# A mixture-of-experts trunk: the busiest expert changes places with the 13th, and that place gets 32 more slots

## The chip, the core and the metric

The kernel runs on one core of a Trainium2 chip. The metric is the device time of one execution in microseconds, a median over several runs. Engines are named as in the profile: PE (TensorE, with PEld its weight loads), DVE (VectorE), ACT (ScalarE), POOL (GpSimd), SP (SyncE, which issues all DMA loads here).

## The reference

One layer on 256 tokens of 1024 features, in float32: a norm, a mixer (differential attention beside a gated linear recurrence), a norm, and a mixture of 32 experts in which each token goes to the four best; then a last norm. The change lies in the experts:

```python
logits = (xt @ w_router).astype(jnp.float32) + b_router
top_v, top_e = lax.top_k(logits, TOP_K)
gates = jax.nn.softmax(top_v, axis=-1)
...
xb = xt[tok]
h = xb @ w_gu[e] + b_gu[e]
y = clamped_swiglu(h) @ w_down[e] + b_down[e]
return y * g[:, None].astype(y.dtype)
```

w_gu[e] is 1024 x 2048 (8 MB) and w_down[e] 1024 x 1024 (4 MB), so one expert has 12.58 MB (in units of 10^6 bytes). 256 tokens times 4 are 1024 places, 32 for an expert on average, and how many an expert really gets depends on the data.

## The kernel before

The first 120 us or so are the mixer and the router. `top4` makes the selection, `posm` holds for each token and expert the token's place in that expert's list, counted from 1 (0 if not selected), `gate` its weight, `cnt` the number of tokens of each expert. Then a loop over the experts runs, fully unrolled, each expert with CAP = 64 slots.

Weights arrive in chunks of 2 MB, six for an expert (`load_chunk`, L180): four of w_gu (h < NU, one DMA each) and two of w_down (two DMAs each). The order is that of `seq`: expert after expert, only for the last two experts all w_gu chunks come first. Ten buffers (`SLOTS`, six in one pool and four single ones) are used in turn; `ahead` (L1086) issues loads on SP up to ten chunks ahead of the use. PE and SP keep the order in which the code is written (`manual_schedule`); DVE, ACT and POOL are ordered by a scheduler.

For one expert e PE does, in this order:

- `gu_mm` (L863): for each 128 features k two products of 512 columns per half, h <- we, xg; 64 slots on half of the array's columns, so the two column halves g go side by side. These are 64 instructions of L875.
- `finish` (`combine`, L936): the products with the gates of the pair of experts before, added to `acc` by DVE.
- `act_t` (L891): transposes of the activation; between them `begin_gu` (L669) opens the next expert's accumulators with the bias.
- `need` (L1050): one half of the gather for the next pair of experts, as products with a 0/1 matrix S.
- `down_mm` (L902): y <- we, actT, 32 instructions of L908.

`swiglu` (L880) on DVE and ACT comes between the first and the third. The matrices S and the gates are built by POOL (`hot_rows`, `gate_rows`), pair by pair; the row `pick` that selects an expert's bias by ACT. After expert LATE = 13 `start_acc` (L1057) adds the residual and the down biases.

An expert with more than 64 tokens needs more than its slots. `plan` (L947), DVE's work at expert 1, counts how many blocks of 64 are missing (`todo_x`) and lists their experts. After the last expert's products and its combine (`fin`, L1145, into the accumulators `fps`) `extras` (L1041) runs nested branches, up to 15: a block (`extra`, L967) reads its expert's number into a register of SP, loads all six chunks of that expert again by that register (tiles wx), gathers, multiplies and adds to `fps`. The trace has one such block. Then `lnc` (the last norm's two rows) is loaded into buffer 5, and the last norm follows: BATCH_NORM_STATS2 on `fps` (L1193), their aggregate, the scaled rows, and the output in four DMAs.

`hint` (L681) marks for PE which way the first of these branches will go, from the count that L1154 loads into a register at the beginning of the last expert.

Of the kernel before, what the change touches and what calls it, by code (L numbers as in the profile page):

```python
# [23 lines left out]
NE = 32  # L24
CAP = 64
NX = 15
ALPHA = 2.0 ** 0.25
EPS = 1e-5
# [3 lines left out]
NW1 = 6  # L32
LATE = 13
NPRE = 4
# [13 lines left out]
def trunk(ctx, tc, x, ln0_g, ln0_b, w_in, conv_w, conv_b, w_rg_a, b_rg_a, w_rg_x, b_rg_x,  # L48
# [129 lines left out]
    seq += [(e, h) for e in (NE - 2, NE - 1) for h in range(NU, NH)]  # L178

    def load_chunk():  # L180


        i = nchunk[0]
        nchunk[0] += 1
        e, h = seq[i]
        w = wtile(f"we{e}_{h}", SLOTS[i % len(SLOTS)])
        if h < NU:
            SP.dma_start(w, w_gu[0, e].rearrange("(d p j) n -> p d (j n)", p=P, j=2)[:, h])
            for j in range(2):
                W[e, 2 * h + j] = w[:, j * 2 * D:(j + 1) * 2 * D]  # L190
            return
        for g in range(2):
            s = w_down[0, e].rearrange("(g b p j) n -> p g b (j n)", g=2, p=P, j=2)[:, g, h - NU]
# [472 lines left out]
    def open_pgu():  # L666
        pgu.append(sgu.enter_context(tc.tile_pool(name="pgu", bufs=3, space=PSUM, reuse_waits="tile")))

    def begin_gu(e, bs=range(2), pk=None):  # L669

        ps = begun.setdefault(e, {})
        if not ps:
            picks[e] = keep.tile([P, 2, CAP], F32R, tag="pick", bufs=2, name=f"pick{e}")
            src = pk[:, :, None] if pk is not None else two.rearrange("p (g c) -> p g c", g=2)[:, :, e:e + 1]
            A.activation(picks[e], src.to_broadcast([P, 2, CAP]), AF.Copy)
        for b in bs:
            ps[b] = pgu[-1].tile([P, 512], F32, tag="gu", name=f"h{e}_{b}")
            PE.matmul(ps[b], picks[e].rearrange("p g w -> p (g w)"), bgs[b], start=True, stop=False,  # L678
                      skip_group_check=True)
# [237 lines left out]
    def gate_rows(e):  # L917

        sg = wk.tile([P, NT, 3 * CAP], F32, tag="sgate", bufs=1, name=f"sgate{e}")
        for i in range(3):  # L920
            for t in range(NT):
                o = e + i % 2
                G.tensor_scalar(sg[:, t, i * CAP:(i + 1) * CAP], iota2[:, 0], posm[:, t, o:o + 1],  # L923
                                gate[:, t, o:o + 1], op0=OP.is_equal, op1=OP.mult)
        return sg
# [15 lines left out]

    start = keep.tile([P, NE], F32, name="start")
    upto = keep.tile([P, NE], F32, name="upto")
    posx = keep.tile([P, NT, NE], F32, name="posx")
    todo_x = keep.tile([1, NX + 1], I32, name="todo_x")

    def plan():  # L947


        xs = wk.tile([P, NE], F32, tag="sg", name="xs")  # L950
        V.tensor_scalar(xs, cnt, float(CAP), None, op0=OP.is_gt)
        for j in range(2, T // CAP):
            V.scalar_tensor_tensor(xs, cnt, float(j * CAP), xs, op0=OP.is_gt, op1=OP.add)
        V.tensor_tensor_scan(upto, ones[:, :NE], xs, 0.0, op0=OP.mult, op1=OP.add)
        V.tensor_sub(start, upto, xs)
        for t in range(NT):
            V.scalar_tensor_tensor(posx[:, t], start, float(CAP), posm[:, t], op0=OP.mult, op1=OP.add)
        le = wk.tile([1, NX, NE], F32, tag="l", bufs=2, name="le")
# [8 lines left out]
    def extra(i):  # L967

        key = f"x{i}"
        ex = nc.values_load(todo_x[0:1, i + 1:i + 2], engines=[ENG.SP], min_val=0, max_val=NE - 1)  # L970
        for h in range(NH):
            w = wtile(f"w{key}_{h}", SLOTS[nchunk[0] % len(SLOTS)] if i == 0 else 0)
            nchunk[0] += 1
            if h < NU:
                SP.dma_start(w, w_gu[0][bass.ds(ex, 1)].rearrange("o (d p j) n -> p (o d) (j n)", p=P, j=2)[:, h])
                for j in range(2):
                    W[key, 2 * h + j] = w[:, j * 2 * D:(j + 1) * 2 * D]
            else:
                src = w_down[0][bass.ds(ex, 1)].rearrange("o (g b p j) n -> p (o g) b (j n)", g=2, p=P, j=2)
                for g in range(2):  # L980
                    c = KT + 2 * (h - NU) + g
                    W[key, c] = w[:, g * 2 * D:(g + 1) * 2 * D]
                    SP.dma_start(W[key, c], src[:, g, h - NU])
        m = wk.tile([P, NE], F32, tag="mx", bufs=1, name=f"m{key}")
# [7 lines left out]
        V.tensor_scalar(pm, pm, -float((i + 1) * CAP), None, op0=OP.add)  # L992
        tmp = wk.tile([P, 2, NE], F32, tag="l", bufs=2, name=f"p{key}")
# [9 lines left out]
        xg = []  # L1003
        for half in range(2):
            xg.append(gather_tile(S, "g", f"{key}_{half}"))
            ps = mc("xg_ps")
# [7 lines left out]
        for t in range(NT):  # L1014
            PE.transpose(ps[:, t * P:(t + 1) * P], sg[:, t], ident)
        gt = wk.tile([P, 2, T], F32, tag="gtT", bufs=1, name=f"gtT{key}")[:, 0]
        A.activation(gt, ps[:, :T], AF.Copy)
# [6 lines left out]
        for b in range(2):  # L1024
            act_t(key, g, b, at[:, 2 * b:2 * b + 2])
        ps = dtiles(key)[0]
# [7 lines left out]
        y = ytile(key, 0)  # L1034
        A.activation(y, ps, AF.Copy)
        for t in range(NT):
            for n in range(2):
                ns = slice(n * CAP, (n + 1) * CAP)
                PE.matmul(fps[t][n], gt[ns, t * P:(t + 1) * P], y[ns], start=False, stop=True, skip_group_check=True)

    def extras(n, i=0):  # L1041
# [8 lines left out]
    def need(i, eng, half):  # L1050
        if i < len(GROUPS):
            es = GROUPS[i]
            if i not in xgs:
                xgs[i] = gather(es, CAP, posm[:, :, es[0]:es[-1] + 1], eng, "g")
            gather_mm(*xgs[i], half)
# [117 lines left out]
    for t in range(NT):  # L1173
        fin(t, gt, y, stop=True)
    extras(nx)
    lnw = wtile("lnc", 5)
# [66 lines left out]
```

## Time and profile before

| what | us |
|---|---|
| median of three runs | 1092.73 (1091.76 to 1093.57) |
| the profiled execution | 1092.81 |
| its span, first to last instruction | 1091.1 |
| PE busy in the span | 1005.0 (92%) |
| DVE, ACT, POOL busy | 281.6, 189.9, 147.2 |
| moved by DMA | 435.02 MB, mean 399 GB/s |

The page's second part cuts the span into 40 slices of 27.3 us. A list of waits has, for each engine and line, what it waited for, the total in us, how often, and the longest; SPq is the queue of SP, with its DMA issues. A row of a window has its ends, its length, and the busy time of PE, PEld, DVE, ACT and POOL with their instructions, the granted clock of PE, the DMA engines' busy share and GB/s. A timeline row has start, duration, engine, line, operation and tiles, and how long the engine stood before. A row by form has a bar, then the busy time and the mean of one instruction in ns, and a second bar with the idle time before. Where the rows of one line are listed, three numbers stand for the shortest, the median and the longest duration in ns. Tile names lose their numbers there: wx and hx belong to the extra block.

### The profile page before, as it was taken

The page shows a single profiled execution, that of the slowest core. Times are in us where ns is not written, and L with a number is a line of the kernel's source. Part 1 is how long each engine was busy: PE and PEld are TensorE (multiplying, and loading weights), DVE is VectorE, ACT ScalarE, POOL GpSimd, SP SyncE. Part 2 cuts the span into 40 slices and gives each one's busy share as a digit, 9 for nine tenths or more (in the row PEclk, how much of TensorE's full clock was granted, in tenths as well). Part 3 has the DMA queues.
Part 4 walks back from the last instruction along what each step waited for, and adds up shares of the span by engine and source line. Part 5 has one row for each costly group of instructions (what it writes and reads, how often), then busy time and mean ns, then how long its engine had stood idle before and what let it go on. Part 6 is the DMA issues. An engine that isn't in the chain of part 4 may idle for free. (4 is left out here: it accounts for less than half of the span.)

```text
span 1091.1 us, 12166 instructions
## 1 busy us (share of the span) xinstructions
PE 1005.0 (92%) x4904; PEld 455.8 (42%) x4904; DVE 281.6 (26%) x634; ACT 189.9 (17%) x429; POOL 147.2 (13%) x221
## 2 busy tenths in 40 slices
PE   8999999999999988989999988888888999888994
PEld 8987633444443332333343333333333333332341
DVE  6978413221211211115121212112011212121123
ACT  6675311111111010110111110100001111110011
POOL 4583202010110100101010101010010101010001
PEclk9999999999999999998999999999999999999997
DMA  8967799999999999999999999999999999999982
GB/s 282 323 258 327 294 412 428 427 426 425 424 427 424 424 427 424 424 425 426 427 427 424 426 426 423 427 426 422 425 425 426 427 426 425 426 425 427 424 357 80
DMA packets 48255, 435.02 MB, mean 399 GB/s; under 512 B 6493, under 2 KB 6558, under 8 KB 14528
## 3 DMA queue, kind: packets, MB, share of 16 engines
q1 hardware_dynamic: 48192, 434.17, 95.6%
q8 instruction: 41, 0.67, 0.3%
q14 instruction: 22, 0.18, 0.0%
HBM read 433.10 MB, written 1.05 MB: 398 GB/s over the span
## 5 line engine op out<-in xcount | busy, mean ns | idle before, releaser
L875 PE MATMUL h<-we,xg 128*64 128x512 f32 x2048 | 457.9, 595 | 55.8 <-DMA we<-in_w_gu_dram 55.1
L875 PEld LDWEIGHTS h<-we,xg 128*64 128x64 f32 x2048 | 145.0, 137 | 361.9 <-issue 290.7
L908 PE MATMUL y<-we,actT 128*64 128x512 f32 x1024 | 228.9, 599 | 0.0
L885 DVE TENSOR_SCALAR g<-h 128x256 f32<-128x256 f32 x64 | 27.2, 425 | 674.1 <-PE h L875 674.1
L923 POOL TENSOR_SCALAR sgate<-iota,posm,gate 128x64 f32<-128x64 f32 x96 | 54.6, 587 | 767.8 <-PE gt_ps L931 766.8
L908 PEld LDWEIGHTS y<-we,actT 128*64 128x64 f32 x1024 | 70.8, 137 | 135.3 <-issue 131.4
L886 ACT ACTIVATE sg<-g 128x256 f32<-128x256 f32 x64 | 26.6, 416 | 578.8 <-DVE g L885 578.8
L783 PE MATMUL xg_ps<-S,n 128*128 128x128 f32 x512 | 65.7, 282 | 0.0
L783 PEld LDWEIGHTS xg_ps<-S,n 128*128 128x128 f32 x512 | 64.1, 196 | 2.3 <-issue 0.8
L937 PE MATMUL cb<-ysb,gtT 128*128 128x512 f32 x116 | 57.5, 618 | 0.0
L1134 ACT ACTIVATE ysb<-y 128x512 f32<-128x512 f32 x30 | 16.3, 594 | 140.7 <-PE y L908 140.7
L939 DVE TENSOR_TENSOR acc<-acc,cb 128x512 f32<-128x512 f32 x58 | 39.5, 681 | 0.0
L388 PE MATMUL pj<-xh,hi 128*128 128x256 f32 x128 | 37.3, 291 | 0.0
L388 PE MATMUL pj<-xo,hi 128*128 128x256 f32 x128 | 36.9, 288 | 0.3 <-DVE xo L343 0.3
L388 PE MATMUL pj<-xh,lo 128*128 128x256 f32 x128 | 36.6, 286 | 0.0
L937 PEld LDWEIGHTS cb<-ysb,gtT 128*128 128x128 f32 x116 | 19.6, 189 | 37.4 <-issue 13.9
L251 POOL TENSOR_TENSOR lo<-win,hi 128x1024 fp32r<-128x1024 f32 x11 | 33.0, 3020 | 12.7 <-PE pj L388 12.6
L791 DVE TENSOR_SCALAR xg<-xg_ps,gb 128x128 f32<-128x128 f32 x64 | 21.9, 404 | 45.8 <-PE xg_ps L783 45.8
L896 PE MATMUL actT_ps<-ident,g 128*128 128x128 f32 x128 | 29.1, 309 | 3.4 <-DVE g L889 2.3
L678 PE MATMUL h<-bgu,pick 128*128 128x512 f32 x64 | 30.3, 476 | 0.3 <-PE actT_ps L896 0.3
L897 ACT ACTIVATE actT<-actT_ps 128x256 f32<-128x256 f32 x64 | 24.5, 382 | 30.0 <-PE actT_ps L896 28.3
L896 PEld LDWEIGHTS actT_ps<-ident,g 128*128 128x128 f32 x128 | 21.4, 203 | 19.5 <-DVE g L889 6.9
(301 smaller groups left out, 736.4 us busy)
## 6 DMA issues: line engine op xcount, KB each, us to landing
we<-in_w_gu_dram SPq DMA_DIRECT2D x128, 2048.0 KB, 18.0
we<-in_w_down_dram SPq DMA_DIRECT2D x127, 1024.0 KB, 29.4
win<-in_w_in_dram SPq DMA_DIRECT2D x8, 1024.0 KB, 10.3
wx<-in_w_gu_dram SPq DMA_DIRECT2D x4, 2048.0 KB
wout<-in_w_out_dram SPq DMA_DIRECT2D x4, 1024.0 KB
wx<-in_w_down_dram SPq DMA_DIRECT2D x4, 1024.0 KB, 27.1
win<-in_w_in_dram SPq DMA_DIRECT2D x4, 512.0 KB, 8.1
x<-in_x_dram SPq DMA_DIRECT2D x4, 256.0 KB, 3.1
```

Of the source, the lines that this page charges most:

```text
L251: return (eng or V).tensor_sub(lo, src, f32(hi))
L388: PE.matmul(ps[m // 2][:, m % 2], a, b, start=k == 0 and m % 2 == 0 and i == 0, stop=k == KT - 1 and i == 2, skip_group_check=True)
L678: PE.matmul(ps[b], picks[e].rearrange("p g w -> p (g w)"), bgs[b], start=True, stop=False, skip_group_check=True)
L783: PE.matmul(ps[:, (k % 4) * n:(k % 4 + 1) * n], pairs(n1[t])[:, k // 2, k % 2], S[:, t], start=start, stop=t == NT - 1, skip_group_check=True)
L875: PE.matmul(ps[b][g * CAP:(g + 1) * CAP], xg[k // 4][:, k % 4, o:o + CAP], W[e, k][:, c0:c0 + 512], start=False, stop=k == KT - 1, skip_gr ...
L885: V.tensor_scalar(g[:, ns], ps[b][:, 0::2], 7.0, None, op0=OP.min)
L886: A.activation(s, g[:, ns], AF.Sigmoid, scale=1.702)
L896: PE.transpose(ps[:, j * P:(j + 1) * P], gj[:, j], ident)
L908: PE.matmul(ps[n][gs], at[:, 2 * b + j, g * CAP:(g + 1) * CAP], w_dn(e, 2 * g + b, j, n * 512, 512), start=c + j == 0, stop=c + j == 4, sk ...
L923: G.tensor_scalar(sg[:, t, i * CAP:(i + 1) * CAP], iota2[:, 0], posm[:, t, o:o + 1], gate[:, t, o:o + 1], op0=OP.is_equal, op1=OP.mult)
L937: PE.matmul(pp, gt[:, n, t * P:(t + 1) * P], y, start=True, stop=True)
L939: V.tensor_add(acc[t][:, ns], acc[t][:, ns], pp)
```

## The change

Experts 0 to 3 stay fixed (FIXED). Of the others the busiest is found on DVE (`star`, a row with a single 1; the first of them if there are several), and it changes places with number 12 (WIDE): the list `who` tells which expert stands at which place, and copies of `posm`, `gate` and `two` with these two columns exchanged (`at_place`) serve gather, gates and bias. SP reads `who` into a register for each place from 4 on, and loads w_gu and w_down by that register.

Place 12 gets 32 slots more (OCAP): for tokens 65 to 96 of that expert a second, narrower set of products runs on the same weights, in six branches that are taken if the expert has more than 64 tokens. `wide_begin` ahead of expert 12's w_gu products gathers the tokens, transposes their gates and opens an accumulator `hw`; `wide_mm(d)` follows on each w_gu chunk, with 32 slots on a quarter of the array's columns, four at a time; `wide_act` is their activation; `wide_down`, after expert 12's down products, multiplies by w_down and adds to `acc`.

The plan of extra blocks counts the starred expert with 32 tokens less and moves to expert 4 (`plan_rest`). `extras` moves ahead of the last expert's down products. `start_acc` moves from after expert 13 to after expert 21. The extra block itself uses other buffers.

```diff
-LATE = 13
+LATE = 21
...
+FIXED = 4
+WIDE = 12
...
+    def by_register(ex):
+
+        return (w_gu[0][bass.ds(ex, 1)].rearrange("o (d p j) n -> p (o d) (j n)", p=P, j=2),
+                w_down[0][bass.ds(ex, 1)].rearrange("o (g b p j) n -> p (o g) b (j n)", g=2, p=P, j=2))
...
+                rows[e] = by_register(nc.values_load(who[0][0:1, e:e + 1], engines=[ENG.SP], min_val=0, max_val=NE - 1))
...
+        gu, down = rows_of(e)
         if h < NU:
-            SP.dma_start(w, w_gu[0, e].rearrange("(d p j) n -> p d (j n)", p=P, j=2)[:, h])
+            SP.dma_start(w, gu[:, h])
...
+        m8 = wk.tile([P, 8], F32, tag="mx", bufs=1, name="m8")
+        V.max(m8, cnt[:, FIXED:])
+        V.memset(star[:, :FIXED], 0.0)
+        V.tensor_scalar(star[:, FIXED:], cnt[:, FIXED:], m8[:, 0:1], None, op0=OP.is_equal)
...
+        sw = star[:, None, :].to_broadcast([P, 2, NE])
+        for name in ("pos", "gate", "two"):
+            src = at_place(name, 0)
+            dst = swapped[name] = wk.tile([P, 2, NE], F32, tag=f"{name}_s", bufs=1, name=f"{name}_s")
+            d = tmp(2)
+            V.tensor_sub(d, src[:, :, WIDE:WIDE + 1].to_broadcast([P, 2, NE]), src)
+            V.tensor_mul(d, d, sw)
+            V.tensor_add(dst, src, d)
+            d = tmp(2)
+            V.tensor_mul(d, src, sw)
+            V.tensor_reduce(dst[:, :, WIDE], d, axis=AX.X, op=OP.add)
...
+        V.scalar_tensor_tensor(past, star, -float(OCAP), cnt, op0=OP.mult, op1=OP.add)
+        V.tensor_scalar(xs, past, float(CAP), None, op0=OP.is_gt)
...
+    def at_wide(label, *parts):
+
+        with tc.If(wide["n"] > CAP, preferred_fallthrough_block=True, label=label):
+            for part in parts:
+                part()
+
+    def wide_begin():
+
+        e = WIDE
+        pm = wk.tile([P, NT, 1], F32, tag="pm", name="pmw")
+        V.tensor_scalar(pm, at_place("pos", e)[:, :, e:e + 1], -float(CAP), None, op0=OP.add)
+        xg = gather([e], OCAP, pm, V, "o")
+        for half in range(2):
+            gather_mm(*xg, half)
...
+    def wide_mm(d):
+        for k in (2 * d, 2 * d + 1):
+            for g in range(P // OCAP):
+                PE.matmul(wide["h"][g * OCAP:(g + 1) * OCAP], wide["xg"][k // 4][:, k % 4], W[WIDE, k][:, g * 512:(g + 1) * 512],
+                          start=False, stop=k == KT - 1, skip_group_check=True)
+
+    def wide_act():
+        wide["g"] = wk.tile([P, 256], F32, tag="go", bufs=1, name="gw")
+        swiglu("w", [wide["h"]], 0, wide["g"])
+
+    def wide_down():
+        ng, n = P // OCAP, 256
+        ao = wk.tile([P, 2, P], F32, tag="l", name="actTw")
+        act_t("w", wide["g"], 0, ao)
+        ps = mc("yw_ps")
+        for k in range(KT):
+            for g in range(ng):
+                m, j = k // 2, k % 2
+                PE.matmul(ps[g * OCAP:(g + 1) * OCAP, :n], ao[:, j, m * OCAP:(m + 1) * OCAP],
+                          w_dn(WIDE, m, j, g * n, n), start=k == 0, stop=k == KT - 1, skip_group_check=True)
...
-        g = first(e, lambda i: e == 0 and i == 6 and need(0, V, 1))
+        if e == WIDE:
+            at_wide("wide", wide_begin)
+        g = first(e, lambda i: (e == 0 and i == 6 and need(0, V, 1),
+                                e == WIDE and i in (4, 8, 12) and at_wide(f"wide{i}", lambda: wide_mm(i // 4 - 1))))
+        if e == WIDE:
+            at_wide("wide16", lambda: wide_mm(3), wide_act)
         if e == 1:
             plan()
+        if e == FIXED:
+            plan_rest()
+        if e == WIDE - 1:
+            wide["n"] = nc.values_load(who[0][0:1, NE:NE + 1], engines=[ENG.PE, ENG.DVE, ENG.Activation],
+                                       min_val=0, max_val=T)
...
+            if e == WIDE:
+                at_wide("wide_down", wide_down)
             ahead(e, NH)
...
+    extras(nx)
     for j in range(4):
         down_mm(e, at2, ps, j)
...
-    extras(nx)
```

In the order of the changed program below, numbers stand behind the names where rows would read alike; the lines L1116 are the six branches (`at_wide`), L1180 the nested extras, L196 the read of `who`, and ISA rows are register steps.

More of the change, by code (lines that the diff above doesn't have):

```diff
@@ L178, in trunk, with rows_of @@
     seq += [(e, h) for e in (NE - 2, NE - 1) for h in range(NU, NH)]
+    def by_register(ex):
+        return (w_gu[0][bass.ds(ex, 1)].rearrange("o (d p j) n -> p (o d) (j n)", p=P, j=2),
+                w_down[0][bass.ds(ex, 1)].rearrange("o (g b p j) n -> p (o g) b (j n)", g=2, p=P, j=2))
+    rows = {}
+    def rows_of(e):
+        if e not in rows:
+            if e < FIXED:
+                rows[e] = (w_gu[0, e].rearrange("(d p j) n -> p d (j n)", p=P, j=2),
+                           w_down[0, e].rearrange("(g b p j) n -> p g b (j n)", g=2, p=P, j=2))
+            else:
+                rows[e] = by_register(nc.values_load(who[0][0:1, e:e + 1], engines=[ENG.SP], min_val=0, max_val=NE - 1))
+        return rows[e]
+    who = []
     def load_chunk():
@@ L192, in load_chunk @@
         for g in range(2):
-            s = w_down[0, e].rearrange("(g b p j) n -> p g b (j n)", g=2, p=P, j=2)[:, g, h - NU]
+            s = down[:, g, h - NU]
             c = KT + 2 * (h - NU) + g
@@ L667, in open_pgu, with at_place @@
         pgu.append(sgu.enter_context(tc.tile_pool(name="pgu", bufs=3, space=PSUM, reuse_waits="tile")))
+    swapped = {}
+    def at_place(name, e):
+        if e >= FIXED:
+            return swapped[name]
+        return {"pos": posm, "gate": gate, "two": two.rearrange("p (g c) -> p g c", g=2)}[name]
     def begin_gu(e, bs=range(2), pk=None):
@@ L673, in begin_gu @@
             picks[e] = keep.tile([P, 2, CAP], F32R, tag="pick", bufs=2, name=f"pick{e}")
-            src = pk[:, :, None] if pk is not None else two.rearrange("p (g c) -> p g c", g=2)[:, :, e:e + 1]
+            src = pk[:, :, None] if pk is not None else at_place("two", e)[:, :, e:e + 1]
             A.activation(picks[e], src.to_broadcast([P, 2, CAP]), AF.Copy)
@@ L939, in combine @@
         V.tensor_add(acc[t][:, ns], acc[t][:, ns], pp)
[L942 to L945, printed above, removed]
-    def plan():
+    star = wk.tile([P, NE], F32, tag="star", bufs=1, name="star")
+    start = wk.tile([P, NE], F32, tag="start", bufs=1, name="start")
+    upto = wk.tile([P, NE], F32, tag="upto", bufs=1, name="upto")
+    posx = wk.tile([P, NT, NE], F32, tag="posx", bufs=1, name="posx")
@@ L969, in extra @@
         key = f"x{i}"
-        ex = nc.values_load(todo_x[0:1, i + 1:i + 2], engines=[ENG.SP], min_val=0, max_val=NE - 1)
+        gu, down = by_register(nc.values_load(todo_x[0:1, i + 1:i + 2], engines=[ENG.SP], min_val=0, max_val=NE - 1))
         for h in range(NH):
-            w = wtile(f"w{key}_{h}", SLOTS[nchunk[0] % len(SLOTS)] if i == 0 else 0)
+            w = wtile(f"w{key}_{h}", SLOTS[nchunk[0] % len(SLOTS)] if i == 0 else (2, 1, 4, 5)[(6 * i + h) % 4])
             nchunk[0] += 1
             if h < NU:
-                SP.dma_start(w, w_gu[0][bass.ds(ex, 1)].rearrange("o (d p j) n -> p (o d) (j n)", p=P, j=2)[:, h])
+                SP.dma_start(w, gu[:, h])
                 for j in range(2):
@@ L982, in extra @@
                     W[key, c] = w[:, g * 2 * D:(g + 1) * 2 * D]
-                    SP.dma_start(W[key, c], src[:, g, h - NU])
+                    SP.dma_start(W[key, c], down[:, g, h - NU])
         m = wk.tile([P, NE], F32, tag="mx", bufs=1, name=f"m{key}")
@@ L1002, in extra @@
                             op0=OP.is_equal, op1=OP.mult)
-        xg = []
+        xgt = ytile(key, 0).rearrange("p (h k c) -> p h k c", h=2, k=4)
+        xg = [xgt[:, half] for half in range(2)]
         for half in range(2):
-            xg.append(gather_tile(S, "g", f"{key}_{half}"))
             ps = mc("xg_ps")
@@ L1039, in extra @@
                 PE.matmul(fps[t][n], gt[ns, t * P:(t + 1) * P], y[ns], start=False, stop=True, skip_group_check=True)
+    wide = {}
+    def at_wide(label, *parts):
[9 more added lines that the diff above has]
+            gather_mm(*xg, half)
+        sg = wk.tile([P, NT, P], F32, tag="sg", name="sgatew")
+        for t in range(NT):
+            V.tensor_scalar(sg[:, t, :OCAP], iota2[:, 0, 0:OCAP], pm[:, t, 0:1], at_place("gate", e)[:, t, e:e + 1],
+                            op0=OP.is_equal, op1=OP.mult)
+            V.tensor_copy(sg[:, t, OCAP:].rearrange("p (g c) -> p g c", c=OCAP),
+                          sg[:, t, None, :OCAP].to_broadcast([P, P // OCAP - 1, OCAP]))
+        ps = mc("gtw_ps")
+        for t in range(NT):
+            PE.transpose(ps[:, t * P:(t + 1) * P], sg[:, t], ident)
+        gt = wk.tile([P, T], F32, tag="gto", bufs=1, name="gtTw")
+        A.activation(gt, ps[:, :T], AF.Copy)
+        pick = wk.tile([P, 2, P], F32R, tag="l", name="pickw")
+        V.memset(f32(pick), 0.0)
+        for b in range(2):
+            V.tensor_copy(pick[:, b].rearrange("p (g b c) -> p b g c", g=2, b=2)[:, b], picks[e][:, :, :OCAP])
+        h = mc("hw")
+        for b in range(2):
+            PE.matmul(h, pick[:, b], bgs[b], start=b == 0, stop=False, skip_group_check=True)
+        wide.update(xg=xg[1], gt=gt, h=h)
@@ new lines, in wide_mm @@
+    def wide_mm(d):
[16 more added lines that the diff above has]
+                          w_dn(WIDE, m, j, g * n, n), start=k == 0, stop=k == KT - 1, skip_group_check=True)
+        y = wk.tile([P, n], F32, tag="l", name="yw")
+        A.activation(y, ps[:, :n], AF.Copy)
+        for g in range(ng):
+            gs, ns = slice(g * OCAP, (g + 1) * OCAP), slice(g * n, (g + 1) * n)
+            pp = mc(f"cbw{g}").rearrange("p (t n) -> p t n", t=NT)
+            for t in range(NT):
+                PE.matmul(pp[:, t], wide["gt"][gs, t * P:(t + 1) * P], y[gs, :], start=True, stop=True,
+                          skip_group_check=True)
+            for t in range(NT):
+                V.tensor_add(acc[t][:, ns], acc[t][:, ns], pp[:, t])
@@ L1053, in need @@
             if i not in xgs:
-                xgs[i] = gather(es, CAP, posm[:, :, es[0]:es[-1] + 1], eng, "g")
+                xgs[i] = gather(es, CAP, at_place("pos", es[0])[:, :, es[0]:es[-1] + 1], eng, "g")
             gather_mm(*xgs[i], half)
```

42 lines of the change are left out of this document (32 added, 10 removed).

## The prediction

> **What bounds the kernel now.** I read the page's slices first, then the two lists of waits, then windows of the expert loop, then the timeline of the end. The slices show what the core's DMA engines moved:
>
> ```profile
> DMA  8967799999999999999999999999999999999982
> GB/s 282 323 258 327 294 412 428 427 426 425 424 427 424 424 427 424 424 425 426 427 427 424 426 426 423 427 426 422 425 425 426 427 426 425 426 425 427 424 357 80
> ```
>
> From the sixth slice (136 us) to the next to last the queue runs at about 426 GB/s without a dip. One expert has four w_gu loads of 2 MB and two w_down chunks of 2 MB (12.58 MB), so one expert takes 12.58 / 0.426 = 29.5 us of the stream. The waits of TensorE, and then of the DMA queue:
>
> ```profile
> PE h L875 <- DMA we<-in_w_gu_dram: 55.1, 51, 1.3
> SPq L188 <- DMA we<-in_w_gu_dram: 442.2, 100, 6.1
> ```
>
> TensorE waits for weights 51 times, and the queue that issues loads waits for its own earlier loads, not for TensorE. So the loop is bound by the stream of weights, and TensorE has slack. How much, and where, stands in these windows (length, TensorE busy first, GB/s last):
>
> ```profile
> 165.00:215.00 50.00, 48.99 (x242) 20.02 (x240) 10.42 (x32) 6.15 (x17) 5.99 (x10) 1.00 1.01 428
> 325.00:350.00 25.00, 25.00 (x119) 9.70 (x119) 5.66 (x14) 2.48 (x6) 3.33 (x8) 1.00 1.01 427
> 350.00:375.00 25.00, 24.19 (x116) 9.11 (x115) 2.80 (x8) 2.74 (x8) 0.00 (x0) 1.00 1.00 422
> 375.00:498.00 123.00, 109.88 (x518) 44.47 (x516) 21.93 (x53) 14.82 (x38) 12.13 (x24) 1.00 1.01 426
> 500.00:525.00 25.00, 23.66 (x77) 7.39 (x78) 9.12 (x16) 1.08 (x2) 0.85 (x3) 0.80 1.01 423
> 525.00:550.00 25.00, 25.00 (x122) 10.14 (x120) 4.29 (x10) 3.30 (x9) 0.00 (x0) 1.00 1.01 425
> 600.00:625.00 25.00, 23.54 (x114) 9.44 (x112) 5.66 (x14) 3.37 (x8) 4.99 (x10) 1.00 1.01 427
> 600.00:994.00 394.00, 352.62 (x1644) 138.36 (x1640) 65.35 (x158) 43.21 (x109) 33.32 (x66) 1.00 1.01 426
> ```
>
> Until about 367 us TensorE works off weights that lay ready when the loop began. From then it is idle for 13.1 of 123 us, 10.7%, or 3.1 us in each expert's 29.5 us. At 500 us start_acc (after expert 13) delays it by some 10 us; it is then full until 600, where idle time returns, and the stream never fell. A delay of TensorE inside the loop is thus free as long as loads continue into free buffers and enough experts follow. What isn't free is the end:
>
> ```profile
> 1031.84 7.09 PE L908 MATMUL y<-we,actT 128*64 128x512 f32 x32
> 1038.96 0.60 ACT L1171 ACTIVATE ysb<-y 128x512 f32<-128x512 f32 x1 [6.41 <-PE y L908]
> 1039.61 3.70 PE L1147 MATMUL fin<-ysb,gtT 128*128 128x512 f32 x8 [0.68 <-ACT ysb L1171]
> 1043.14 3.87 PE L783 MATMUL xg_ps<-Sx,n 128*128 128x64 f32 x32
> 1048.63 13.95 PE L875 MATMUL hx<-wx,xgx 128*64 128x512 f32 x64
> 1074.57 1.99 PE L1039 MATMUL fin<-ysbx,gtTx 64*128 64x512 f32 x8 [0.76 <-ACT ysbx L1035]
> 1076.58 1.28 ACT L237 ACT_TABLE_LOAD   x1 [2.06 <-ACTq L1042]
> 1080.75 0.68 DVE L1193 BATCH_NORM_STATS2 st<-fin 128x6 f32<-128x512 f32 x1
> 1081.47 0.21 DVE L235 BATCH_NORM_AGGREGATE mv_ln<-st 128x2 f32<-128x12 f32 x1
> ```
>
> After the last expert's combine (to 1043.3 us) one extra block runs, for an expert with more than 64 tokens, and only then the last norm.
>
> **The tail: what is removed.** The trace shows one extra block, so just one expert is over 64. The reference's router, evaluated on the reference's own inputs, gives 66 selections to expert 25 and at most 50 to any other. Expert 25 is past the first four and 66 is at most 96, so the new place with 96 slots holds it, and the count of extras becomes 0. Then the norm follows the last combine. Its four products (3.70 us for four, 0.93 each) end at about 1040.6, 1041.5, 1042.4 and 1043.3; the last statistics can start at 1043.35 in place of 1080.75. That is 37.4 us, and from there to the end nothing changes: 1091.1 - 37.4 = 1053.7 us. What could be late next: the Sqrt table (1.28 us) loads right after ACT's copy of y at 1039.6, ready at 1041, used at 1042.5; the two lnc rows need buffer 5, free when expert 30's down products end at 1031.8, and are first read after 1044. Both are covered. If lnc were late by some us, so would the end be.
>
> The 12.58 MB of the extra's weights also go, but they were last in the queue, behind what the loop waits for, so they are not a second gain.
>
> **The new branch at the end.** `extras` moves ahead of the last down products. On TensorE, the end of the program before (y and fin are expert 31's last products):
>
> ```order
> L908 MATMUL y_0_5337<-we_5_5296,actT_5434 64x512
> L908 MATMUL y_1_5338<-we_5_5296,actT_5434 64x512
> L1147 MATMUL fin_0_5347<-ysb_0_5474,gtT_5432 128x512
> L1147 MATMUL fin_1_5348<-ysb_1_5475,gtT_5432 128x512
> L1147 MATMUL fin_0_5349<-ysb_0_5474,gtT_5432 128x512
> L1147 MATMUL fin_1_5350<-ysb_1_5475,gtT_5432 128x512
> L1042 COMPARE_AND_BRANCH
> L783 MATMUL xg_ps<-Sx_5523,n_0_1211 128x64
> ```
>
> And the same place in the changed program, where y still belongs to expert 30:
>
> ```order
> L1297 MATMUL fin_0_5845<-ysb_0_5753,gtT_5700 128x512
> L938 MATMUL y_0_5833<-we_5_5750,actT_5824 64x512
> L938 MATMUL y_1_5834<-we_5_5750,actT_5824 64x512
> ...
> L1297 MATMUL fin_1_5846<-ysb_1_5754,gtT_5700 128x512
> L1180 COMPARE_AND_BRANCH
> L813 MATMUL xg_ps<-Sx_5995,n_0_1211 128x64
> ```
>
> The branch now comes before expert 31's 32 down products, and with no extras it jumps over all 15 blocks. The trace has such a far jump, taken once after the one extra, and near ones:
>
> ```profile
> L1042 PEldq COMPARE_BRANCH  x3: 92/203/3937, 1039.8 to 1078.7; - x3
> L1042 ACTq COMPARE_BRANCH  x3: 38/45/49, 1039.5 to 1076.4; - x3
> ```
>
> The far one took TensorE's sequencer 3.94 us, of which about 2.1 us showed (last product 1076.56, DVE released 1078.67); ACT stood 2.06 us. The Trainium skill, in Runtime: NRT & Kernel Launch, section Instruction fetch mechanics, says that a taken branch whose target lies outside the two pages held must first fetch the page; the 2.06 us agree, and by it alone the sum would take the whole 2.1. Here TensorE's products before it wait for nothing, so its sequencer may run ahead, and a hint names the branch. DVE and ACT jump under the 7.09 us of products. I take 1.0 us, between 0 and 2.1.
>
> **Expert 12: what is added on TensorE.** The first chunk of expert 12 before:
>
> ```order
> L875 MATMUL h_0_3057<-we_0_2895,xg_2821 64x512 x2
> L875 MATMUL h_1_3063<-we_0_2895,xg_2821 64x512 x2
> L875 MATMUL h_0_3057<-we_0_2895,xg_2821 64x512 x2
> L875 MATMUL h_1_3063<-we_0_2895,xg_2821 64x512 x2
> L875 MATMUL h_0_3057<-we_1_2897,xg_2821 64x512 x2
> ```
>
> And now (hw is the wide place's own accumulator):
>
> ```order
> L905 MATMUL h_0_3094<-we_0_2897,xg_2959 64x512 x2
> L905 MATMUL h_1_3100<-we_0_2897,xg_2959 64x512 x2
> L1116 COMPARE_AND_BRANCH
> L1151 MATMUL hw<-we_0_2897,xg_3146 32x512 x8
> L1116 UNCONDITIONAL_BRANCH x2
> L905 MATMUL h_0_3094<-we_1_2909,xg_2959 64x512 x2
> ```
>
> Eight products per chunk stand between, so each chunk's buffer is held longer too. The trace shows no product of 32 columns; nearest rows, and the time of a short burst with its change of shape:
>
> ```profile
> L783 PE MATMUL xg_ps<-Sx,n 128*128 128x64 f32 x32 | 3.9, 279 | 0.0
> L1015 PE MATMUL gt_psx<-ident,sgatex 128*128 128x128 f32 x2 | 0.4, 275 | 0.0
> L678 PE MATMUL hx<-bgu,pickx 128*128 128x512 f32 x2 | 0.9, 500 | 0.5 <-ACT gtTx L1017 0.5
> L1039 PE MATMUL fin<-ysbx,gtTx 64*128 64x512 f32 x8 | 2.0, 615 | 0.8 <-ACT ysbx L1035 0.8
> 1028.92 1.94 PE L908 MATMUL y<-we,actT 128*64 128x512 f32 x8
> 1030.78 1.13 PE L1147 MATMUL fin<-ysb,gtT 128*128 128x512 f32 x2
> ```
>
> A call is two instructions here (64 for 32 calls).
> - Begin: gather 3.9, transposes 0.4, bias 0.9, its wait 0.5: 5.7 us. DVE's seven short steps before it run under expert 11's 7 us of down products.
> - wide_mm: 64 instructions. Two 64-wide halves run at once today: 13.95 us for 64. With four strips at once it is 7.0, with two 14.0; neither row is nearer, I take 10.
> - wide_act: four DVE steps and one of ACT delay expert 12's second transposes; 0.5 to 2 us, I take 1.5.
> - wide_down: transposes, their copy and its wait 1.3; 64 instructions of 256 columns, 3.5 (four at once) to 7.5 (64 weight loads at 3.87 / 32 = 0.12); I take 7.0, near the loads, which such short products hardly hide; copy of y 0.8; combine 16 at half of 3.70 / 8, 3.7.
> - Six branches, in and out, at most 0.2 us each way: 2.4 us, at least 0.6. Twelve changes of shape at (1030.78 - 1028.92) - 8 x 0.218 = 0.12 us: 1.4 us.
>
> Sum X = 5.7 + 10 + 1.5 + 12.8 + 3.8 = 33.8 us, from 23 to 39. The skill's TensorE: Matmul & The Clock Gate, section Measured speedup vs the span model, has three strips of 32 columns at 2.38 times one; if four lose in the same ratio (an estimate), wide_mm takes 7.0 x 3 / 2.38 = 8.8 us and X is 32.6. No run here shows it yet.
>
> Of X, 3.1 us fall into expert 12's own idle time: a delay of 31 us. At 10.6% it is worked off in about 290 us. start_acc moves from expert 13 to 21 and adds its 10 us there; 41 us are needed between 520 and 994 us, 50 are there.
>
> **Do the loads go on meanwhile?** Ten chunks of 4.9 us are buffered, and the longest held are expert 12's two down chunks. From 165 to 367 us TensorE worked off about 200 x 10.7% = 21 us of ready weights, and the row 165:215 shows 428 GB/s with that much ready. The slots allow 44 us less what is in use. A delay of 31 lies between 21 and 44; beyond the limit each us of delay is lost for good. I take a loss of 1 us, from 0 to 10.
>
> **Loads by register.** SP now reads an expert's number ahead of the loads of experts 4 to 31. At expert 5:
>
> ```order
> L220 DMA we_5_1935<-in_w_down_dram 128x2048
> L196 TENSOR_LOAD who
> L196 ISA x2
> L210 ISA
> L210 DMA we_0_1938<-in_w_gu_dram 128x4096
> ```
>
> where before the loads followed one another:
>
> ```order
> L188 DMA we_3_1859<-in_w_gu_dram 128x4096
> L198 DMA we_4_1893<-in_w_down_dram 128x2048 x2
> L198 DMA we_5_1896<-in_w_down_dram 128x2048 x2
> L188 DMA we_0_1899<-in_w_gu_dram 128x4096
> L188 DMA we_1_1901<-in_w_gu_dram 128x4096
> ```
>
> The read is queued behind one expert's loads and ahead of the next's. The extra block did the same before; its prices, the shortest time from issue to landing while slots were scarce (150 to 270 us), and the rate while its register-addressed loads ran:
>
> ```profile
> L1154 SPq TENSOR_LOAD <-todo_x x1: 480/480/480, 1016.9 to 1016.9; - x1
> L1154 SPq FUSED_REGOPS  x1: 181/181/181, 1017.5 to 1017.5; - x1
> DMA to landing us min/median/max: 11.9/19.8/27.1
> 1030.00:1050.00 20.00, 18.79 (x90) 8.88 (x88) 4.02 (x18) 3.18 (x8) 0.00 (x0) 1.00 1.01 426
> ```
>
> About 0.7 us per expert, plus a short register step per load, against 12 us or more already issued: nothing, or at most 28 x 0.9 = 25 us if it all showed. The rate by register is the same 426. The list itself: DVE's plan grows in expert 1, some 25 steps of 0.2 us where 12 stood; it pushes the gather's copies back by under 1 us, 10 us before they are read, and `who` is needed a whole expert later. Masks on POOL and ACT read swapped copies with the same operations. All this I cost at nothing.
>
> **Rivals.**
> - The delay outgrows the buffers: X at 39 to 42 or buffers for only 25 us. For it: 31 is beyond the 21 us that the trace proves. 5 to 10 us are lost: 1060 to 1068. Chance 0.20.
> - Every short branch pays the far jump's 3.94 us on leaving, or 32-wide products run one after another: X = 34 + 24 = 58, a delay of 55, and with room for 31 to 37 of it 18 to 24 us lost: 1074 to 1080. Against: the targets lie one instruction on, and 64-wide products overlap today. 0.07.
> - Slower than before: register-addressed loads sustain less over a whole loop than in the one block. 28 experts are 352 MB, 827 us at 426 GB/s; below 407 GB/s the 37 us are eaten. At 400 it is 53 us: 1110. Against: 426 in the row above. 0.04.
> - The change doesn't take: the busiest expert sits in the first four places or passes 96, an extra still runs, 1093. The count above speaks against it. 0.03.
>
> **How the numbers follow.** Span 1053.7 + 1.0 + 1.0 = 1055.7 us. The profiled execution took 1092.81 us at a span of 1091.1, 1.7 more, and the median of the runs is 1092.73, 0.1 less: 1057.3 us. This case has 0.66. Its bounds are 1055.3 (no jump, no loss) and 1060. The range goes 2 us lower, about the spread of the three runs (1091.76 to 1093.57), and up to 1068, which takes in the first rival: 1053.5 to 1068, 0.86 in all. A measurement can tell about 0.2% (2.2 us). Faster: 0.66 + 0.20 + 0.07 = 0.93; same 0.03; slower 0.04.
>
> **What would show it.** No wx loads; the last statistics about 1 us after the last fin product; in expert 12 the branches' products summing to about 34 us; the stream at 425 GB/s through expert 13 and 14; idle time of TensorE back near 800 us and after start_acc by 900. Wrong would be: a dip of GB/s after expert 12, TensorE full to the end, gaps of 2 us or more around the six branches, or landings that grow with the register loads.

## The result, and the profile after

The changed kernel takes 1059.07 us (median of four runs, 1057.42 to 1060.32), the kernel before 1092.98 in four runs of the same comparison (1091.76 to 1093.57): a ratio of 0.969, with an interval of 0.9673 to 0.9707. The profiled execution took 1058.9 us at a span of 1057.2, where 1055.7 was forecast: 33.9 us less than before's 1091.1.

The slices of the page with the rate answer to those of before:

```profile
GB/s 258 305 309 273 302 405 427 424 423 422 423 424 425 426 423 426 422 424 424 423 424 425 426 425 423 423 424 424 422 424 425 425 426 424 424 425 424 427 416 138
```

From the seventh slice to the 39th the rate lies between 416 and 427 GB/s: the stream has no dip in the loop behind its start. The lists of waits, of TensorE and then of the DMA queue (total in us, times, longest):

```profile
PE h L905 <- DMA we<-in_w_gu_dram: 36.9, 35, 1.7
SPq L210 <- DMA we<-in_w_gu_dram: 389.8, 95, 5.6
```

TensorE waits for weights 35 times in place of 51, and the queue still waits for its own loads. The windows around expert 12 and after it (columns as in the prediction):

```profile
450.00:475.00 25.00, 25.00 (x142) 8.81 (x145) 2.67 (x9) 3.16 (x9) 0.00 (x0) 0.93 1.01 425
475.00:500.00 25.00, 22.26 (x162) 10.52 (x156) 7.02 (x18) 4.08 (x11) 0.00 (x0) 0.95 1.01 422
600.00:625.00 25.00, 24.97 (x122) 10.33 (x120) 5.66 (x14) 2.29 (x6) 5.02 (x10) 1.00 1.01 424
625.00:650.00 25.00, 23.73 (x114) 9.88 (x112) 4.29 (x10) 3.04 (x8) 0.00 (x0) 1.00 1.01 422
825.00:850.00 25.00, 22.04 (x107) 8.72 (x107) 2.06 (x5) 2.76 (x8) 0.00 (x0) 1.00 1.01 424
```

TensorE is full after expert 12 until 625 us, then idle time returns: its next wait for weights ends at 641 us, some 160 us earlier than forecast. After start_acc idle time is back by 850. The 22.26 in the second row hold waits of TensorE inside expert 12, not for weights. The granted clock, a mean over each window, was 0.93 and 0.95 here. In shorter windows it is 0.50 from 454 to 456 and from 498 to 500 us, right behind the short products of the wide place's gather and of its combine, and 1.00 between.

Rows of the timeline of the end, from the last combine of the pair before (fin) over expert 31's down products to the first step of the last norm that reads lnc:

```profile
1034.08 1.12 PE L1297 MATMUL fin<-ysb,gtT 128*128 128x512 f32 x2
1035.36 7.09 PE L938 MATMUL y<-we,actT 128*64 128x512 f32 x32
1039.03 0.35 SPq L1329 DMA_DIRECT2D lnc<-in_ln_g_dram  x1
1042.49 0.60 ACT L1322 ACTIVATE ysb<-y 128x512 f32<-128x512 f32 x1 [6.65 <-PE y L938]
1043.11 1.28 ACT L259 ACT_TABLE_LOAD   x1
1043.14 3.70 PE L1297 MATMUL fin<-ysb,gtT 128*128 128x512 f32 x8 [0.70 <-ACT ysb L1322]
1046.88 0.70 DVE L1343 BATCH_NORM_STATS2 st<-fin 128x6 f32<-128x512 f32 x1
1047.74 0.70 DVE L1351 SCALAR_TENSOR_TENSOR acc<-fin,mv_ln,lnc 128x512 f32<-128x512 f32 x1
```

The table loads beneath fin, and nothing of the extra block is left: the last statistics start 0.04 us after the last fin product ends (1043.14 + 3.70). From the start of the 32 products to the end of the span are 1057.2 - 1035.36 = 21.84 us; the prediction's 1053.7 - 1031.84 are 21.86. So this part came out to a few hundredths, and what the span has more, it has ahead of these products: they start at 1035.36 in place of 1031.84, 3.5 us later. Two rows of TensorE's sequencer (the part that reads its instructions) at the far branch show that the jump is no part of that:

```profile
L1180 PEldq COMPARE_BRANCH  x1: 2795/2795/2795, 1029.3 to 1029.3; - x1
L1180 PEldq EVENT_SEMAPHORE  x1: 51/51/51, 1035.3 to 1035.3; - x1
```

It began 6 us ahead of the products, while older ones still ran, and ended at 1032.1. The semaphore behind it, with which the engine's two ways meet again (its join), came at 1035.3: not with the end of the jump but with that of the last older product (1034.08 + 1.12 = 1035.20). Between the start of fin and the start of y lie 1035.36 - 1034.08 = 1.28 us, where before it was 1031.84 - 1030.78 = 1.06: 0.2 us show, and they are the price of the join. The other 3.3 us are a later stream; the loads are shown with the second experiment.

Expert 12 on TensorE, its gather, its first chunks, its wide down products, and then, for comparison, an ordinary expert from 525.66 to 551.30:

```profile
448.56 3.96 PE L813 MATMUL xg_ps<-S,n 128*128 128x32 f32 x32
453.16 5.35 PE L905 MATMUL h<-we,xg 128*64 128x512 f32 x16
458.44 1.92 PE L1151 MATMUL hw<-we,xg 128*32 128x512 f32 x16
460.30 3.65 PE L905 MATMUL h<-we,xg 128*64 128x512 f32 x16
...
489.57 0.51 PE L926 MATMUL actT_psw<-ident,gw 128*128 128x128 f32 x2
490.55 3.66 PE L1166 MATMUL yw_ps<-we,actTw 128*32 128x256 f32 x64 [0.47 <-ACT actTw L927]
...
496.69 1.24 PE L1174 MATMUL cbw<-yw,gtTw 32*128 32x256 f32 x4 [0.81 <-DVE acc L1177]
497.86 15.49 PE L905 MATMUL h<-we,xg 128*64 128x512 f32 x64
525.66 13.90 PE L905 MATMUL h<-we,xg 128*64 128x512 f32 x64
551.30 1.03 PE L905 MATMUL h<-we,xg 128*64 128x512 f32 x4
```

Expert 12 took 497.86 - 448.56 = 49.3 us, an ordinary one 25.6: 23.7 more, and expert 13's products 1.6 more (15.49 against 13.90), at the lowered clock: 25.3 us where 33.8 were forecast. Before the wide products of the first chunk lie 5.35 us of ordinary ones that take 3.65 elsewhere: 7% of 25 us at a clock of 0.93 are as much. The six branches, in and out on TensorE, and the reads by register on SP:

```profile
L1116 PEldq COMPARE_BRANCH  x12: 65/129/186, 444.2 to 496.7; - x12
```

```profile
L196 SPq TENSOR_LOAD <-who x28: 262/272/477, 186.9 to 968.7; - x28
```

### The profile page after: what moved, and what is told of

It is laid out like the page before. It is cut to its first block, busy times and chain, and to the rows that moved or that the text cites. A ratio compares the mean times of both kernels' runs of the same rounds, so it can differ in the third digit from the quotient of the medians.

```text
span 1057.2 us, 12811 instructions
## 1 busy us (share of the span) xinstructions
PE 995.2 (94%) x4942; PEld 456.3 (43%) x4942; DVE 283.8 (27%) x666; ACT 188.8 (18%) x426; POOL 147.3 (14%) x221
## 5 line engine op out<-in xcount | busy, mean ns | idle before, releaser
L953 POOL TENSOR_SCALAR sgate<-iota,pos_s,gate_s 128x64 f32<-128x64 f32 x84 | 47.1, 580 | 735.3 <-PE gt_ps L961 585.4
L813 PE MATMUL xg_ps<-S,n 128*128 128x128 f32 (+1 forms) x544 | 69.7, 282 | 0.1
L813 PEld LDWEIGHTS xg_ps<-S,n 128*128 128x128 f32 x544 | 68.0, 196 | 3.3 <-issue 2.0
L410 PE MATMUL pj<-xh,hi 128*128 128x256 f32 x128 | 37.4, 292 | 0.0
L821 DVE TENSOR_SCALAR xg<-xg_ps,gb 128x128 f32<-128x128 f32 (+1 forms) x68 | 22.9, 399 | 53.6 <-PE xg_ps L813 53.6
L967 PEld LDWEIGHTS cb<-ysb,gtT 128*128 128x128 f32 x116 | 19.6, 189 | 37.4 <-issue 13.9
L823 ACT ACTIVATE xg<-xg_ps,gb 128x128 f32<-128x128 f32 (+1 forms) x68 | 25.4, 452 | 36.1 <-PE xg_ps L813 36.1
## 6 DMA issues: line engine op xcount, KB each, us to landing
we<-in_w_down_dram SPq DMA_DIRECT2D x127, 1024.0 KB, 29.5
```

The lines of the kernel that those rows point to most:

```text
L410: PE.matmul(ps[m // 2][:, m % 2], a, b, start=k == 0 and m % 2 == 0 and i == 0, stop=k == KT - 1 and i == 2, skip_group_check=True)
L813: PE.matmul(ps[:, (k % 4) * n:(k % 4 + 1) * n], pairs(n1[t])[:, k // 2, k % 2], S[:, t], start=start, stop=t == NT - 1, skip_group_check=True)
L967: PE.matmul(pp, gt[:, n, t * P:(t + 1) * P], y, start=True, stop=True)
```

## The experiments

The theory: the gain is the extra block that no longer stands at the end; expert 12's extra work is hidden in TensorE's slack as long as it fits the buffers and enough experts follow; loads by register cost nothing; the far jump is hidden under the last down products. Each rival gives one of these another price. Where no other kernel is named, the edit is to the changed kernel.

**The changed kernel again**, beside the next three.

> The changed kernel unaltered, as the measure for the three others on this chip. My theory of the result: 37.4 us of tail are gone, the stream of weights is 3.3 us late at the end (1.6 us already before the loop, 1.7 us drift within it), the far jump shows 0.2 us, and expert 12's added 25 us cost nothing. Then 1057 to 1060 us again. If the 1.6 us before the loop and the drift were chance of one execution, the median falls to about 1056.

It took 1058.73 us (1057.79 to 1061.37), the kernel before 1091.83: 0.9699 (0.9679 to 0.9718). The gain stands. The five runs of this program differ by up to 3.6 us and the nine of the kernel before by 4.3 (1090.37 to 1094.65), so a microsecond between medians is no finding here.

**Fixed addresses.** All weights are loaded from fixed addresses, with no register. Places 12 and 25 then get each other's weights, so the output of these two experts is another.

```diff
-            if e < FIXED:
+            if e < NE:
```

> All places load their weights by fixed addresses; SP reads no register. Places 12 and 25 then hold each other's tokens with their own weights, so the output of these two experts is left wrong. Theory A (reading who and register addresses on SP slow the stream): the drift of about 0.07 us per expert goes, and the time falls by 1.7 us against the unaltered kernel of this call. Theory B (registers cost nothing, the drift is variation between executions): the same within 0.7 us.

It took 1059.57 us (1056.87 to 1060.58), a ratio of 0.9692 (0.9672 to 0.9712): the registers cost nothing that can be seen. The loads themselves say it more sharply. Where a place has an ordinal, the count is from 1: the wide place, number 12, is the 13th. These are the timeline's rows of SP, the first w_gu issue of the 12th and of the 31st place, in the kernel before, in the changed one, and in this one:

```profile
386.39 5.22 SPq L188 DMA_DIRECT2D we<-in_w_gu_dram  x2
950.35 5.23 SPq L188 DMA_DIRECT2D we<-in_w_gu_dram  x2
```

```profile
387.84 0.33 SPq L210 DMA_DIRECT2D we<-in_w_gu_dram  x1
953.66 0.34 SPq L210 DMA_DIRECT2D we<-in_w_gu_dram  x1
```

```profile
389.01 0.33 SPq L210 DMA_DIRECT2D we<-in_w_gu_dram  x1
954.67 0.33 SPq L210 DMA_DIRECT2D we<-in_w_gu_dram  x1
```

At the 31st place the changed kernel is 953.66 - 950.35 = 3.3 us late, the whole of what was missing above. Of that, 1.45 us were there at the 12th place and 1.86 came over the 19 experts between: 563.96 us before, 565.82 after (0.3%), and 565.66 with fixed addresses. So something makes the changed kernel's stream a little longer, and it isn't the registers.

**The kernel before, with no extra block.** The count of blocks is set to 0, so expert 25's two tokens past 64 are left out.

```diff
-        V.tensor_copy(lst[:, 0:1], upto[:1, NE - 1:])
+        V.memset(lst[:, 0:1], 0.0)
```

> The kernel before, with the count of extra blocks set to 0: the two tokens past expert 25's 64 slots are left out, all else stays, the extras' branch after the last combine too. My theory: 1091.1 - 37.4 = 1053.7 us of span, plus 2 to 3 us for the far jump that now shows behind the last combine, plus 1.7: 1057.5 to 1058.5. So nearly the whole gain of the change is the extra block's absence, and all the rest of the change costs 1 to 2 us net. Rival (most of the gain is in something else, the order of the end or the stream): 1065 or more.

It took 1057.64 us (1057.39 to 1061.52), 0.9692 (0.9671 to 0.9713). This is the whole gain, by one constant; what the rest of the change does is to keep the two tokens without the block. Its span was 1055.7, and the timeline of its end shows why it isn't 1053.7:

```profile
1039.53 3.70 PE L1147 MATMUL fin<-ysb,gtT 128*128 128x512 f32 x8 [0.68 <-ACT ysb L1171]
1043.36 1.29 DVE L1193 BATCH_NORM_STATS2 st<-fin 128x6 f32<-128x512 f32 x2 [3.75 <-PEq L1042]
1045.44 0.68 DVE L1193 BATCH_NORM_STATS2 st<-fin 128x6 f32<-128x512 f32 x1
```

DVE waits until 1043.36 for TensorE's sequencer at the branch, though the first fin product was done at about 1040.7 (1.17 us after its start, as in the changed kernel: 1044.31 - 1043.14). The last statistics start at 1045.44 where fin ends at 1043.23: at its old place the branch costs 2.2 us, and 1053.7 + 2.2 is the span within 0.2. That is the 2 to 3 us that were expected, but not for the reason given. The sequencers' rows at the branch, TensorE and DVE:

```profile
L1042 PEldq COMPARE_BRANCH  x1: 402/402/402, 1039.7 to 1039.7; - x1
L1042 DVEq EVENT_SEMAPHORE  x1: 21/21/21, 1042.5 to 1042.5; - x1
L1042 PEldq EVENT_SEMAPHORE  x1: 51/51/51, 1043.3 to 1043.3; - x1
```

TensorE's jump took 0.40 us and was over at 1040.1, beneath fin. Its join came at 1043.3, with the end of the last fin product, and DVE's statistics wait for that join. So they can't start one by one as the four products end, as in the changed kernel, but all after the last one; from the first to the last of them are 1045.44 - 1043.36 = 2.08 us. DVE itself was through its own jump only at 1042.5. Without TensorE's join its last statistics would thus have started at about 1042.5 + 2.08 = 1044.6 (an estimate), still some 1.3 us late.

**The branch behind the last combine.** The jump goes back to where it stood.

```diff
-    extras(nx)
     for j in range(4):
         down_mm(e, at2, ps, j)
...
         fin(t, gt, y, stop=True)
+    extras(nx)
```

> The changed kernel with the extras' branch put back behind the last combine, where it was before the change. My theory: the jump of 2.8 us that TensorE's sequencer took under products is now in front of the last norm, on TensorE, DVE and ACT alike: 2 to 3 us longer than the unaltered kernel. Rival (the hint fetches the target in time, or the sequencers reach the branch early enough anyway): the same within 0.7 us.

It took 1060.68 us (1060.1 to 1062.29), 2.0 us more than the changed kernel beside it. The tail, again by its timeline:

```profile
1041.22 3.70 PE L1297 MATMUL fin<-ysb,gtT 128*128 128x512 f32 x8 [0.68 <-ACT ysb L1321]
1045.04 0.35 SPq L1329 DMA_DIRECT2D lnc<-in_ln_g_dram  x1
1047.13 0.68 DVE L1343 BATCH_NORM_STATS2 st<-fin 128x6 f32<-128x512 f32 x1
1049.14 0.75 DVE L1351 SCALAR_TENSOR_TENSOR acc<-fin,mv_ln,lnc 128x512 f32<-128x512 f32 x1 [1.09 <-DMA lnc<-in_ln_g_dram]
```

The statistics are held as in the experiment before: the last start at 1047.13, fin ends at 1044.92, 2.2 us. TensorE's jump took 0.39 us here, from 1041.4, and its join came at 1045.0. Beside them the load of lnc is issued only at 1045.04, behind that join, and its first reader waits 1.09 us for it. So the end is 3.3 us longer; the stream was earlier in this execution (its y products began at 1033.45), which takes part of it back. To move the branch ahead of 7 us of queued products is thus worth some 3 us in this kernel, by its tail.

**No wide branch.** The six branches are left out, and with them the two tokens.

```diff
-        with tc.If(wide["n"] > CAP, preferred_fallthrough_block=True, label=label):
-            for part in parts:
-                part()
+        return
```

> The changed kernel without the six branches at expert 12: the two tokens past 64 are left out, everything else stays. My theory: the added 25 us of TensorE's time there are worked off in idle time that would be waiting for weights anyway, so the time is the same within 0.7 us of the changed kernel (1057 to 1060). Rival (loads fall behind for some us while TensorE is late, a loss for good): 2 us shorter or more.

It took 1057.54 us (1057.25 to 1060.47), 0.9671 (0.9645 to 0.9696). By the medians that is 1.2 and 1.5 us less than the two of the changed kernel, by the ratios 2 to 3, with intervals that overlap; so the times alone don't part the theory (within 0.7) from the rival (2 or more). The trace does, for the profiled execution: its span, 1055.7, is 1.5 us shorter than the changed kernel's, but its stream was already 387.84 - 386.14 = 1.7 us earlier at the 12th place, ahead of any wide work. From there to the 31st place it took 952.22 - 386.14 = 566.08 us, as long as the changed kernel's: the wide branches don't lengthen it.

**start_acc after expert 13 again.**

```diff
-LATE = 21
+LATE = 13
```

> start_acc back after expert 13, right behind the wide place: TensorE is then late by 25 - 3 + 10 = 32 us at once. My theory from the buffers (ten chunks of 4.9 us less what is in use, 31 to 37 us): a loss of 0 to 1 us, 1057 to 1061. Rival (buffers carry only the 21 to 25 us that the trace of before shows): the stream of loads dips after expert 13 and 7 to 11 us are lost for good, 1066 to 1070.

It took 1059.7 us (1057.92 to 1060.7), 0.9683 (0.9649 to 0.9716): no loss that can be seen. The window in which both delays stand together:

```profile
500.00:525.00 25.00, 24.32 (x91) 9.88 (x88) 11.82 (x26) 2.30 (x6) 5.00 (x10) 0.87 1.00 423
```

The granted clock was 0.87, which added to the delay, and the stream still ran at 423. Expert 14's products started at 536.05 us, and without a delay they would have at 475.56 (expert 13 before) + 29.5 = 505.1: 31 us fit the buffers. The rival with room for 21 to 25 us is out.

**The wide products three and six times.** The wide slots then sum each product three (six) times, so their result is another; only the length of the work matters.

```diff
-        for k in (2 * d, 2 * d + 1):
+        for k in (2 * d, 2 * d + 1) * 3:
```

> Each wide_mm runs its products three times (the wide tokens' result is wrong, all else stays): 15 us more at expert 12, a delay of 25 + 15 - 3 = 37 us in all. My theory (room for 31 to 37 us): a loss of 0 to 6 us, 1058 to 1065, and GB/s dips a little in the windows behind expert 12. Rival 1 (room for 21 to 25): 12 to 16 us lost, 1071 to 1075. Rival 2 (room for the whole 44 us): no loss, 1057 to 1060.

Three times: 1058.84 us (1058.35 to 1061.62), 0.9683 (0.965 to 0.9717), no loss. Expert 13 started at 510.66 us in place of 475.56, a delay of 35.1.

> Each wide_mm runs its products six times: 37 us more, a delay of 25 + 37 - 3 = 59 us. My theory (room for 31 to 37 us): 22 to 28 us are lost for good, 1081 to 1087; GB/s falls clearly behind expert 12, and TensorE, late by 31 to 37, works that off by the end. Rival 1 (room for 21 to 25): 34 to 38 us lost, 1093 to 1097. Rival 2 (a delay of TensorE is free anywhere in the loop as long as idle time follows, whatever the buffers): 59 + 10 against 52 us of idle time, 17 us late, 1076.

Six times: 1080.93 us (1080.73 to 1082.49), 0.988 (0.9847 to 0.9914). The windows at the limit, of the kernel with three and then of the one with six:

```profile
500.00:525.00 25.00, 23.21 (x154) 8.94 (x152) 3.37 (x10) 0.79 (x3) 0.00 (x0) 0.93 0.99 404
```

```profile
475.00:500.00 25.00, 25.00 (x212) 7.38 (x206) 0.00 (x0) 0.00 (x0) 0.00 (x0) 1.00 0.99 407
500.00:525.00 25.00, 24.05 (x166) 9.24 (x162) 5.90 (x14) 3.72 (x10) 0.00 (x0) 1.00 0.43 167
525.00:550.00 25.00, 23.21 (x152) 9.01 (x149) 4.95 (x14) 1.36 (x4) 0.00 (x0) 0.93 0.79 311
```

With six the stream stands for want of free buffers while TensorE is busy: against 424 GB/s these three windows lack 1.0, 15.2 and 6.7 us of stream, 22.8 in all. The span was 1079.4, 22.4 us more than the unaltered kernel's 1057.0 beside the first experiments. These two rows of the timeline give the delay:

```profile
460.05 10.51 PE L1151 MATMUL hw<-we,xg 128*32 128x512 f32 x96
533.67 6.63 PE L905 MATMUL h<-we,xg 128*64 128x512 f32 x22
```

Expert 13 started 533.67 - 475.56 = 58.1 us late, and 58.1 - 22.4 = 35.7 us were carried. With three times, 35.1 cost nothing at the end, though 404 in place of 426 GB/s over 25 us is a first 1.3 us of lost stream. The room is thus some 34 to 36 us; the changed kernel uses 22.3 of it (497.86 - 475.56).

**The wide place at 28.**

```diff
-WIDE = 12
+WIDE = 28
```

> The wide place at 28 in place of 12; all else stays. My theory: the 25 us that the wide place adds are free only where idle time of TensorE follows. Behind place 28 there are the idle times of experts 28 to 31 alone, some 3 us each for three of them, so 25 - 9 = 16 us show at the end: 1073 to 1078. Rival (what the loads bind is free wherever it stands, since ten chunks are buffered): 1057 to 1061.

It took 1070.84 us (1067.71 to 1073.77), 0.9802 (0.9769 to 0.9835), 12 us over the changed kernel, a little under what was expected. The start and end of place 28 on TensorE, and the start of place 31's products:

```profile
923.24 3.96 PE L813 MATMUL xg_ps<-S,n 128*128 128x32 f32 x32
970.72 13.95 PE L905 MATMUL h<-we,xg 128*64 128x512 f32 x64
1014.44 5.80 PE L905 MATMUL h<-we,xg 128*64 128x512 f32 x26
```

and the same start of place 31's in the changed kernel:

```profile
1005.08 7.09 PE L905 MATMUL h<-we,xg 128*64 128x512 f32 x32
```

Place 28 took 47.5 us, 21.8 more than an ordinary one (no lowered clock here), and at place 31 there were 1014.44 - 1005.08 = 9.4 us left: 12.4 were worked off at three places. The profiled execution, the shortest of the four, ended 8.8 us after the changed kernel's, and so shows where the time went; why the others took up to 6 us more, no trace shows. The same work is thus free at place 12 and isn't near the end.

## Why the prediction was right, point by point

- **The tail.** 37.4 us was right to a few hundredths, and the kernel before without its block shows that the whole gain comes from there.
- **The far jump.** 1.0 us was taken, between 0 and 2.1; 0.2 showed. The sequencer did run ahead, as said, but the 0.2 are not left over from the jump: where its record took 0.40 and 0.38 us in place of 2.8 (with no wide branch, and with the products six times), the same 1.28 us lie between fin and y. The 2.2 us at the old place equal the 2.1 read from the trace of before by chance. There TensorE's join came 2.0 us after the last product, behind a jump of 3.94 us; here it came with the last product, and the order of the statistics made the 2.2. What does show of the jump in the two kernels with the branch at its old place is that the next step of DVE and ACT came 2.5 to 3.1 us behind it. The rule of the Trainium skill, in Runtime: NRT & Kernel Launch, Instruction fetch mechanics, agrees with these stops; the 2.1 us it would have put into the sum were hidden.
- **Expert 12.** The mechanism was right and the size was off: 33.8 against 25.3 us, of which some 3.5 are the lowered clock (7% and 5% of 25 us, 2% of the next), that no step had foreseen. Without it, as at place 28, it is 21.8, below the least that was given, 23. By parts: the begin 453.16 - 448.56 = 4.6 (5.7 forecast); the wide products 4 x (460.30 - 458.44) = 7.4 (10); their activation's wait 0.95 (1.5); the wide down products with the combine 497.86 - 489.57 = 8.3 (12.8), since 64 instructions took 3.66 and not 7.0: the weight loads set no limit. What is left for the branches and changes of shape, beyond what these parts hold of them, is 0.6 us (3.8).
- **Four strips at once.** 1.86 us for 16 instructions is 0.116 each, where the 64-wide pairs take 0.218: 1.88 times the rate, and 2.0 times in the burst of 96 (10.51 / 96 = 0.109). The estimate from the Trainium skill's TensorE: Matmul & The Clock Gate, Measured speedup vs the span model (8.8 us), was nearer than my 10, but the loss that it carried over from three strips didn't appear.
- **The delay.** It was absorbed, as said. The idle time per expert was set too low: 19 experts took 563.96 us of stream, 29.7 each, and a pair of experts without waits takes 577.51 - 525.66 = 51.85 us, 25.9 each, so 3.8 us are free and not 3.1. The window's idle share misses that a chunk's products started alone take 3.65 us, and in a run of four chunks 13.90 / 4 = 3.48: 0.7 us per expert of the busy time is gone when the chunks run on without a wait. So 22 us were worked off by 640 us and not by 800.
- **Room in the buffers.** Given as 21 to 44; it is 34 to 36. The rival at 0.20 needed room for only 25, or 39 us of extra work; the first is excluded, and the second, all but reached by the threefold products, cost nothing at the end yet. The rival of serial products and dear branches is out too: 0.13 us per branch. The 1.0 us taken for a loss was nothing that can be seen.
- **Loads by register.** Nothing, as said.
- **lnc.** The prediction had its buffer free at 1031.8; it was issued at 1039.03, since SP stood at its own join behind the branch until 1038.8. It was read at 1047.74 without a wait, 8.7 us later where at least 12 were said, and with the branch at its old place the cover is gone.
- **What was missed.** The later stream, 3.3 us, stands in no step. Its share ahead of the 12th place (1.45 us) varies between executions ahead of anything that the experiments changed: the third place's first w_gu load was issued at 138.74 us here, at 138.24 in the repeat, at 137.03 with the branch at its old place, and at 137.04 in the kernel before. The other 1.9 us were there in every kernel of the changed family but the sixfold one, whose stream stood: 565.3 to 566.1 us between the two loads, in one trace each, against 563.96 and 564.54 in the kernel before and its version without the block. Registers, wide branches and start_acc's place are excluded by the runs above; that the tiles lie elsewhere in memory wasn't tried, and the cause stays open.

The two allowances of 1 us each were for things that cost 0.2 and nothing, and part of the 3.3 us fell where they had made room. So the forecast missed the span by 1.5 us where its terms, put right, would have missed it by 3.3: that nearness is luck.

## What to carry to other kernels

Rare work that stood serially at the end is best done where the loop has slack, early: what it may cost there is the room in the buffers (35 us here), and how far from the end it must lie is its delay over the free time per round (22 / 3.8, six experts). A branch goes ahead of a long run of queued products, together with the loads that follow it, and not between the last products and the work that takes them up one by one: behind the branch that work waited here for the last product, though TensorE's jump took 0.4 us.

## What the runs showed of the hardware

- Four strips of 32 columns run at once, in float32 products of 512 columns: 0.109 us per instruction in a burst of 96, against 0.43 from one whole-array product of fin to the next (rows of its weight loads, 1044.97 and 1045.40) and 0.218 in the 64-wide pairs. That is the full fourfold rate.
- Sixty-four products of 256 columns on four strips, each with a weight load of its own, take 3.66 us, 0.057 each.
- A near branch, into a wide part or out of it, took TensorE's sequencer 0.065 to 0.186 us, DVE's and ACT's 0.034 to 0.055. The far one's record on TensorE took 0.38 to 0.50 us in five traces, 2.6 to 2.9 in five and 3.94 in that of the kernel before; what makes it short or long no run tells. In all but the last, TensorE's join came within 0.1 us of the end of its last older product.
- The granted clock fell to 0.50 for some 3 us where dense products follow expert 12's short ones (0.93 as the mean of the first window), and not at place 28, where the same products in the same order ran at 1.00; with start_acc behind expert 13 it was 0.87 in the window from 500 us. What decides it no run here tells.
